# A two-layer diffusion backbone step: modulation loads on GpSimd's queue, one more modulation piece as VectorE sums, and eight instead of seven products in three groups of layer 0's MLP

## The chip, the cores and the metric

The kernel runs on one core of a Trainium2 chip. The metric is the device time of one execution in microseconds, the median over several runs.

## What is computed

The reference is one inference step through two post-norm layers, in float32, for 128 context tokens and 512 latent tokens (five tiles of 128) of width 1024:

```python
mod = silu(c) @ w_mod[l] + b_mod[l]          # 1024 -> 6 x 1024, one vector for latent, one for context tokens
sh1, sc1, g1, sh2, sc2, g2 = split(mod, 6)
u = x * (1 + sc1) + sh1
m = mixer(u)                                 # in-projection; SSD scan | short conv | differential attention; out-projection
x = layer_norm(ALPHA * x + g1 * m)
h = x * (1 + sc2) + sh2
f = square(relu(h @ w_up)) @ w_down          # 1024 -> 4096 -> 1024
x = layer_norm(ALPHA * x + g2 * f)
```

The six parts of `mod` are called pieces 0 to 5. Piece 5 is `g2`, the gate of the MLP's output, and is needed first when a layer's last MLP group is summed up. A layer's pieces 0 and 1 are needed before its in-projection, pieces 3 and 4 before its MLP.

## The kernel before

Every product of activations and weights is made in three float32r products: both operands are split into a rounded high part and a rest, and high x high, low x high and high x low are added in PSUM. For weights, ScalarE writes the high part and VectorE the rest (`split_unit`, L351); the activations lie transposed as `XH` and `XL`, eight row blocks by 640 tokens.

The code is written as straight Python over layers, groups and tiles. A framework turns it into one fixed order per engine: it takes, for each engine, the instruction of the best priority among those ready in its own estimate of the times, and puts in the waits. Priority is the place in the program, moved back by `LATE` = 100 places inside `high_priority(offset=-LATE)`. On the chip each engine and each DMA queue (SP's, ScalarE's, GpSimd's) then goes through its list in order.

**Modulation in layer 0.** Pieces 0 and 1 of layer 0 are made at the start. `mod_steps` (L186) makes pieces 2 to 5 of layer 0 (`PIECES`) on TensorE beside the z, sa and sb projections (the gate stage): per step two row blocks of `w_mod` are loaded (`wm`, 512 KB each, SP's queue, L200) and multiplied with a 32-column stationary operand. A piece has four such steps, and three for its tail (`mod_tail`, L160: copy, four transposes to a column layout, bias; after pieces 2 and 5 a transpose and a DMA of the gate to `gdram`).

**Modulation in the MLPs.** `mod_steps_sum` (L219) makes pieces 0 to 4 of layer 1 beside layer 0's MLP, and piece 5 of layer 1 beside layer 1's (`PIECES_MLP`). Here VectorE does the work: each of eight row blocks k and two column halves is loaded as `ws` (128x512, 256 KB, ring of 3, L232, SP's queue) and for each of the two token kinds added to a sum with the conditioning value as a per-partition scalar (L248; ScalarE for k = 0, L246). Four matmuls with ones close a piece over the partitions (L253), and `mod_tail` follows. A piece takes 19 steps, and one step of loads stands before the first piece. The sums `ma` are a ring of two, which the gate rows `grow` (L1147) use too.

**The pace.** `fill` takes steps from the list `fillers`. `spread(n)` (L268) adds n to an account and takes its whole part. It is called once for each of the 17 evacuations of the gate stage with `FZ` = 2.6, and in the MLP for each of 8 evacuations of an up-projection with `FU` = .6 and each of 10 of a down-projection with `FD` = 1.2. What is left is taken by `fill_all` in `before_last` (L1435).

**The MLP.** The 4096 hidden columns go in eight groups of 512 (L1450). Group 0 uses `up_block` (L1255): a plain product, 4 column tiles x 2 token halves x 8 row blocks x 3 = 192 matmuls of 320 tokens. Groups 1 to 7 use `fast_pair` (L1328) twice: seven products in place of eight (the Strassen-Winograd scheme on halves of rows and tokens), 2 x 7 x 4 x 3 = 168 matmuls. It forms differences of weights on VectorE and splits seven operands of 128x512 per pair, where a plain block splits four units of 128x1024 in all; its results are put together with three more VectorE adds per pair. The sums of tokens that it multiplies are made once (`token_sums`, L1289), and one quarter of `XH` and `XL` is overwritten by a difference (`token_sums_in_place`, L1310) after group 0's `up_block`, which needs the old content. Each group then has its down-projection (`dn_block`, L1404), 120 matmuls of 512 columns over four PSUM banks. In layer 0 ScalarE copies each result to a `part` buffer (ring of 3) and a DMA on GpSimd's queue adds it to `acc` (L1486); in layer 1 VectorE adds it from PSUM (L1489). Weight units live in a ring of five (`hi`, `lo`), their raw loads in a ring of three on SP's queue (L348, L1337).

`before_last` runs after the first pair of group 7: it takes all remaining steps, asks for the gate rows on GpSimd's queue (L1148), multiplies `acc` by them and adds the saved residual (L1439 to L1443).

Of the kernel before, what the change touches and what calls it, by code (L numbers as in the profile page):

```python
# [16 lines left out]
P = 128  # L17
# [15 lines left out]

RK, RZ, RY, RS, RW = 4, 4, 1.5, 2, 1

FZ, FU, FD = 2.6, .6, 1.2

PIECES, PIECES_MLP = (2, 3, 4, 5), (tuple((1, i) for i in range(5)), ((1, 5),))

DF, EK = 3, 2  # L40

# [17 lines left out]
def build(ctx: ExitStack, tc: tile.TileContext, I, O):  # L59
    nc = tc.nc  # L60
    V, S, G, T = nc.vector, nc.scalar, nc.gpsimd, nc.tensor
# [157 lines left out]
    def mod_steps_sum(pieces, pool):  # L219

        loads = [(l, pc, k, h) for l, pc in pieces for k in range(KT) for h in range(2)]
        got = {}

        def small(name):
            return pool.tile([P, 512], F32, tag="ws", name=name, bufs=3)

        def load():
            if loads:
                l, pc, k, h = at = loads.pop(0)
                w = got[at] = small(f"ws{l}_{pc}_{k}_{h}")  # L230
                c0 = pc * 1024 + h * 512
                nc.sync.dma_start(out=w, in_=I["w_mod"][l, k * P:(k + 1) * P, c0:c0 + 512])  # L232

        for _ in range(3):
            load()
        yield
        for l, pc in pieces:
            acc = [pool.tile([P, 1024], F32, tag="ma", name=f"ma{l}_{pc}_{s}", bufs=2) for s in range(2)]
            for k in range(KT):
                for h in range(2):  # L240
                    w = got.pop((l, pc, k, h))
                    with tc.high_priority(offset=-LATE):
                        for s in range(2):
                            a = acc[s][:, h * 512:(h + 1) * 512]
                            if k == 0:
                                act(a, w, scale=cst_c[:, k, s:s + 1])  # L246
                            else:
                                stt(a, w, cst_c[:, k, s:s + 1], a, ALU.mult, ALU.add)  # L248
                    load()
                    yield  # L250
            ps = ps_tp(f"pmod{l}_{pc}")
            for g in range(4):
                mm(ps[32 * g:32 * g + 32, :], one, acc[g // 2][:, (g % 2) * 512:(g % 2 + 1) * 512], True, True)  # L253
            yield from mod_tail(l, pc, ps, small(f"mrow{l}_{pc}"), False)
            yield
# [12 lines left out]
    def spread(n):  # L268
        due[0] += n
        fill(int(due[0]))  # L270
        due[0] -= int(due[0])
# [344 lines left out]
    for l in range(DEPTH):  # L616
# [131 lines left out]
        k = k_tile(NT)  # L748
# [506 lines left out]
        def up_block(g, b, ah, al):  # L1255
            blk = load_block(f"up{l}_{g}_{b}", w_up, 0, [(g * hg + b * 512, 512)])

            def ev_up(ct, half, ps):
                nm = f"relu{l}_{g}_{b}_{ct}_{half}"
                o, m, r = half * H, H, room(nm)  # L1260
                squared(r, ah[4 * b + ct][:, o:o + m], al[4 * b + ct][:, o:o + m], ps)
                spread(FU)

            ch_block(f"up{l}_{g}_{b}", blk, ev_up, na=H)

# [62 lines left out]
        def fast_pair(g, j, ah, al):  # L1328

            i = 2 * j  # L1330
            nm = f"{l}_{g}_{j}"
            c0 = g * hg + i * P
            raw = []
            for k in range(2):
                r = raw_tile(f"rup{nm}_{k}").rearrange("p (k c) -> p k c", k=4)
                src = w_up[512 * k:512 * k + 512, c0:c0 + 256]
                nc.sync.dma_start(out=r, in_=src.rearrange("(k p) c -> p k c", p=P))  # L1337
                raw.append(r)
            b11, b12, b21, b22 = (raw[k][:, :, P * c:P * c + P] for k in range(2) for c in range(2))
            w = {}  # L1340

            def unit(n, pool, bufs, t):
                return [pool.tile([P, n, 512], F32R, tag=x, name=f"{x}{nm}_{t}", bufs=bufs)
                        .rearrange("p i (k c) -> p i k c", k=4) for x in (("hi", "lo") if n == 2 else ("h1", "l1"))]

            b = unit(2, wp, 5, "b")
            for e, (n, x) in enumerate((("B11", b11), ("B21", b21))):
                act(b[0][:, e], x)
                tt(b[1][:, e], x, f(b[0][:, e]), ALU.subtract)
                w[n] = b[0][:, e], b[1][:, e]  # L1350
            t1, t2, t3, t4 = (flat(f"t{nm}_{i}").rearrange("p (a b) -> p a b", a=4) for i in range(4))
            sums = {"T1": (t1, b12, b11), "T2": (t2, b22, t1), "T3": (t3, b22, b12), "T4": (t4, b21, t2)}
            for ns in (("T2", "T1"), ("T3", "T4")):
                b = unit(2, wp, 5, ns[0])
                for n in sorted(ns):
                    tt(*sums[n], ALU.subtract)
                for e, n in enumerate(ns):
                    act(b[0][:, e], sums[n][0])
                    tt(b[1][:, e], sums[n][0], f(b[0][:, e]), ALU.subtract)
                    w[n] = b[0][:, e], b[1][:, e]  # L1360
            b = unit(1, op, 2, "c")
            act(b[0][:, 0], b22)
            tt(b[1][:, 0], b22, f(b[0][:, 0]), ALU.subtract)
            w["B22"] = b[0][:, 0], b[1][:, 0]

            def product(ps, wn, xn, more=False):

                for k in range(4):
                    wh, wl = (x[:, k] for x in w[wn])
                    xh, xl = quarter[xn](k)  # L1370
                    T.matmul(ps, lhsT=wh, rhs=xh, start=k == 0 and not more, stop=False, skip_group_check=more)  # L1371
                    T.matmul(ps, lhsT=wh, rhs=xl, start=False, stop=False, skip_group_check=more)  # L1372
                    T.matmul(ps, lhsT=wl, rhs=xh, start=False, stop=k == 3, skip_group_check=more)  # L1373

            def out(r, ct, half, src=None):
                spread(FU)
                o = H * half
                squared(r, ah[i + ct][:, o:o + H], al[i + ct][:, o:o + H], src)

            def bank(p, n):  # L1380
                return p(n + nm)[:, :H]


            px, pz, py = bank(ps_mm, "px"), bank(ps_tp, "pz"), ps_b2(f"py{nm}")[:, 0, :H]
            s1, p5, u = room("s1" + nm), flat("p5" + nm)[:, :H], room("u" + nm)
            product(px, "B11", "A11")
            act(s1, px)
            product(pz, "T1", "S1")
            act(p5, pz)
            product(px, "T2", "S2", True)  # L1390
            act(u, px)
            product(pz, "B22", "S4", True)
            tt(u, u, pz, ALU.add)
            out(u, 1, 0)
            product(px, "T3", "S3", True)
            tt(p5, p5, px, ALU.add)
            out(p5, 1, 1)
            product(py, "B21", "A12")
            tt(s1, s1, py, ALU.add)
            out(s1, 0, 0)  # L1400
            product(px, "T4", "A22", True)
            out(room("c21" + nm), 0, 1, px)
# [47 lines left out]
        for g in range(ng):  # L1450
            ah, al = a_tiles(g, hg // P)
            if g == 1:
                fillers.append(mod_steps_sum(PIECES_MLP[l], op))
            if g:
                for j in range(2):
                    fast_pair(g, j, ah, al)
                    if g == ng - 1 and j == 0:
                        before_last()
            else:
                for b in range(hg // 512):  # L1460
                    up_block(g, b, ah, al)
                    if g == 0 and b == 0:
                        with tc.high_priority(offset=-LATE):
                            for t, mv in later:
                                affine(rows, t, mv)
                                G.dma_start(out=mid[l][t * P:(t + 1) * P, :], in_=res[t])
                        rp_end.close()
                        sp, sp_end = open_pool("sp", "right")
                        with tc.high_priority(offset=-LATE):
                            token_sums()  # L1470
                token_sums_in_place()
            for cbi in range(2):
                blk = load_block(f"dn{l}_{g}_{cbi}", w_down, g * hg, [(cbi * 512, 512)], nu=hg // 256)
                cs = slice(cbi * 512, (cbi + 1) * 512)
# [4 lines left out]
                def ev_dn(t, ps, cbi=cbi, cs=cs, g=g):  # L1479
                    if g == 0:  # L1480
                        act(acc[t][:, cs], ps)
                        spread(FD)
                    elif g < ng - 1 and not end:
                        part = op.tile([P, 512], F32, tag="part", name=f"part{l}_{g}_{cbi}_{t}", bufs=3)
                        act(part, ps)
                        G.dma_start(out=acc[t][:, cs], in_=part, accum_op=ALU.add)  # L1486
                        spread(FD)
                    elif g < ng - 1:
                        tt(acc[t][:, cs], acc[t][:, cs], ps, ALU.add)  # L1489
                        spread(FD)  # L1490
                    else:
                        quiet = end and t in order[:-1]
                        residual(t, cbi, ps, None, not quiet)
# [86 lines left out]
```

## Time and profile before

| | |
|---|---|
| runs | 1637.12, 1631.19, 1635.31 us; median 1635.31 |
| the profiled execution | 1628.37 us |
| its span, first to last instruction | 1626.6 us, mean granted TensorE clock 0.995 |
| busy | TensorE 1563.3 us (96%), VectorE 1203.7 (74%), ScalarE 883.2 (54%), GpSimd 109.1 (7%) |
| layer 0: gate stage, out-projection, MLP begin at | 210.0, 341.4, 395.6 us |
| layer 1: gate stage, MLP begin at | 1040.3, 1183.6 us |

PE is TensorE's matmuls and PEld its weight loads, DVE VectorE, ACT ScalarE, POOL GpSimd, SP the queue of SyncE. Matmuls overlap, so the time of one step is read from the distance of two starts, not from the duration of a row. "x -> y" in a row names the tile written and the tiles read (out<-in), and L with a number the line of the kernel; helpers such as `mm` (L112), `act` (L97), `tt` (L100) and `stt` (L109) give one line to many places, so that tiles tell them apart. In a row of a wait, the engine and line that waited stand first, and after the arrow what released it.

### The profile page before, as it was taken

What the parts mean: (1) busy time and instruction counts of PE and PEld (TensorE: products, weight loads), DVE (VectorE), ACT (ScalarE), POOL (GpSimd) and SP (SyncE); (2) the same over time, 40 slices, a digit from 0 to 9 for tenths busy, and PEclk for the clock granted to TensorE, in tenths of its full rate; (3) what the DMA queues carried; (4) which work ended last, traced back from release to release, by engine and by line L of the source; (5) the groups of instructions that cost most, each with busy time, mean ns of one, the idle gap of its engine ahead of it and who ended that gap; (6) DMA issues with size and microseconds to landing.
All of it is one profiled execution on the core that took longest, in us unless ns stands there. A gap on an engine that the chain in (4) does not pass through costs nothing.

```text
span 1626.6 us, 24095 instructions
## 1 busy us (share of the span) xinstructions
PE 1563.3 (96%) x8944; PEld 1352.6 (83%) x8944; DVE 1203.7 (74%) x2216; ACT 883.2 (54%) x1886; POOL 109.1 (7%) x162
## 2 busy tenths in 40 slices
PE   6999999999999999898999999999999999999997
PEld 3799956787988888788887999798798889988985
DVE  2588865678994877667587788898799665565677
ACT  3368743436665465465455577564486355434543
POOL 0000000001002211210300000000000000000011
PEclk9999999999999999999999999999999999999999
DMA  9641177543256866774735510524334243122332
GB/s 323 176 163 53 53 249 256 183 151 139 79 182 143 226 178 168 192 186 142 185 130 169 197 40 14 181 98 148 112 133 131 81 130 90 66 69 88 104 113 81
DMA packets 142533, 227.71 MB, mean 140 GB/s; under 512 B 12236, under 2 KB 73424, under 8 KB 142416
## 3 DMA queue, kind: packets, MB, share of 16 engines
q1 hardware_dynamic: 122608, 179.46, 34.5%
q0 software_dynamic: 12256, 28.32, 7.8%
q10 hardware_dynamic: 7552, 18.40, 3.1%
q8 instruction: 70, 1.15, 0.3%
q14 instruction: 47, 0.39, 0.1%
HBM read 191.95 MB, written 18.46 MB: 129 GB/s over the span
## 4 chain that ended last, share of the span: by engine, by line
PE 59%; issue 22%; DVE 8%; DMA 4%; POOL 3%; ACT 3%; SPq 1%; POOLq 0%; DVEq 0%; ACTq 0%
PE dn_t L112 13%; PE wo_t L112 5%; PE sa_c L112 4%; PE xb_c L112 3%; PE kv_t L112 3%; PE z_t L112 3%; POOL acc L1486 3%; PE pt L112 2%; PE pmod L112 2%; PE xa_c L112 2%; PE px L1371 2%; PE px L1372 2%; PE px L1373 2%; PE dq_t L112 2%; PE sb_c L112 1%
## 5 line engine op out<-in xcount | busy, mean ns | idle before, releaser
L112 PE MATMUL dn_t<-hdn,al 128*128 128x512 f32 x640 | 252.0, 394 | 0.8 <-DVE al L100 0.8
L112 PE MATMUL dn_t<-hdn,ah 128*128 128x512 f32 x640 | 252.1, 394 | 0.0
L112 PE MATMUL dn_t<-ldn,ah 128*128 128x512 f32 x640 | 251.4, 393 | 0.0
L112 PEld LDWEIGHTS dn_t<-hdn,ah 128*128 128x128 f32 x640 | 120.1, 188 | 29.4 <-issue 0.8
L112 PEld LDWEIGHTS dn_t<-hdn,al 128*128 128x128 f32 x640 | 120.2, 188 | 28.3 <-DVE al L100 1.1
L112 PEld LDWEIGHTS dn_t<-ldn,ah 128*128 128x128 f32 x640 | 120.2, 188 | 27.4
L109 DVE SCALAR_TENSOR_TENSOR ma<-ws,cstat,ma 128x512 f32<-128x512 f32 x168 | 118.9, 748 | 28.6 <-DMA ws<-in_w_mod_dram 21.3
L100 DVE TENSOR_TENSOR ldn<-rdn,hdn 128x1024 fp32r<-128x1024 f32 x64 | 78.0, 1222 | 30.6 <-ACT hdn L97 30.5
L97 ACT ACTIVATE hi_T<-t 128x512 fp32r<-128x512 f32 x112 | 67.2, 626 | 56.7 <-DVE t L100 33.6
L100 DVE TENSOR_TENSOR lo_T<-t,hi_T 128x512 fp32r<-128x512 f32 x112 | 73.9, 687 | 30.2 <-ACT hi_T L97 30.1
L100 DVE TENSOR_TENSOR acc<-acc,dn_t 128x512 f32<-128x512 f32 x80 | 54.1, 684 | 49.6 <-PE dn_t L112 49.4
L1371 PE MATMUL px<-XH,hi_T 128*128 128x320 f32 x224 | 71.4, 319 | 12.6 <-ACT u L97 10.0
L97 ACT ACTIVATE hi_b<-rup 128x512 fp32r<-128x512 f32 x56 | 33.3, 623 | 78.2 <-PE dn_t L112 71.3
L97 ACT ACTIVATE hdn<-rdn 128x1024 fp32r<-128x1024 f32 x64 | 67.0, 1050 | 16.2 <-PE px L1372 13.7
L1486 POOL DMA_DIRECT2D acc<-part x60 | 51.3, 907 | 334.1 <-ACT part L97 253.3
L1372 PE MATMUL px<-XL,hi_T 128*128 128x320 f32 x224 | 69.7, 311 | 0.0
L1373 PE MATMUL px<-XH,lo_T 128*128 128x320 f32 x224 | 69.6, 310 | 0.0
L97 ACT ACTIVATE part<-dn_t 128x512 f32<-128x512 f32 x60 | 34.8, 595 | 63.0 <-PE dn_t L112 44.0
L112 PE MATMUL wo_t<-hwo,XH 128*128 128x512 f32 x160 | 63.8, 398 | 1.5 <-ACT XH L97 1.5
L112 PE MATMUL wo_t<-hwo,XL 128*128 128x512 f32 x160 | 63.6, 397 | 0.0
L112 PE MATMUL wo_t<-lwo,XH 128*128 128x512 f32 x160 | 63.2, 395 | 0.0
L97 ACT ACTIVATE pe<-sc,zs 128x640 f32<-128x640 f32 (+1 forms) x80 | 56.8, 711 | 7.5 <-DVE ams L106 3.1
(419 smaller groups left out, 4603.8 us busy)
## 6 DMA issues: line engine op xcount, KB each, us to landing
rup<-in_w_up_dram SPq DMA_DIRECT2D x64, 512.0 KB
rdn<-in_w_down_dram SPq DMA_DIRECT2D x64, 512.0 KB
ws<-in_w_mod_dram SPq DMA_DIRECT2D x96, 256.0 KB
wm<-in_w_mod_dram SPq DMA_DIRECT2D x32, 512.0 KB
acc<-part POOLq DMA_DIRECT2D x60, 256.0 KB, 4.6
Ab<-adram SPq DMA_DIRECT2D x10, 1024.0 KB
rwo<-in_w_out_dram SPq DMA_DIRECT2D x16, 512.0 KB
wb<-in_w_mod_dram SPq DMA_DIRECT2D x12, 512.0 KB
```

Source lines behind the costliest of these rows:

```text
L97: S.activation(out=out, in_=in_, func=func, **kw)
L100: V.tensor_tensor(out=out, in0=a, in1=b, op=op)
L109: V.scalar_tensor_tensor(out=out, in0=a, scalar=s, in1=b, op0=op0, op1=op1, **kw)
L112: T.matmul(out, lhsT=l, rhs=r, start=start, stop=stop)
L1371: T.matmul(ps, lhsT=wh, rhs=xh, start=k == 0 and not more, stop=False, skip_group_check=more)
L1372: T.matmul(ps, lhsT=wh, rhs=xl, start=False, stop=False, skip_group_check=more)
L1373: T.matmul(ps, lhsT=wl, rhs=xh, start=False, stop=k == 3, skip_group_check=more)
L1486: G.dma_start(out=acc[t][:, cs], in_=part, accum_op=ALU.add)
```

## The change

Three things change. The `ws` loads go out on GpSimd's queue. Piece 5 of layer 0 leaves `PIECES` and becomes the first piece that `mod_steps_sum` makes beside layer 0's MLP. And in layer 0 groups 1 to 3 use `up_block`; `fast_pair` begins at group 4 (`FAST`), and the in-place difference is made in group 3. The paces depend on the group: 1.3 per evacuation before `FAST[l]` and .65 from there on, for up and down alike; `FZ` is 2.

```diff
-FZ, FU, FD = 2.6, .6, 1.2
-
-PIECES, PIECES_MLP = (2, 3, 4, 5), (tuple((1, i) for i in range(5)), ((1, 5),))
+FZ, FU, FD = 2, (1.3, .65), (1.3, .65)
+
+FAST = (4, 1)
+
+PIECES, PIECES_MLP = (2, 3, 4), (((0, 5),) + tuple((1, i) for i in range(5)), ((1, 5),))
...
@@ mod_steps_sum
-                nc.sync.dma_start(out=w, in_=I["w_mod"][l, k * P:(k + 1) * P, c0:c0 + 512])
+                G.dma_start(out=w, in_=I["w_mod"][l, k * P:(k + 1) * P, c0:c0 + 512])
...
@@ up_block's ev_up, fast_pair's out
-                spread(FU)
+                spread(FU[g >= FAST[l]])
...
@@ the loop over groups
-            if g:
+            if g >= FAST[l]:
                 for j in range(2):
                     fast_pair(g, j, ah, al)
...
-                token_sums_in_place()
+                if g == FAST[l] - 1:
+                    token_sums_in_place()
...
@@ ev_dn, three places
-                        spread(FD)
+                        spread(FD[g >= FAST[l]])
```

## Rows read from the trace of the kernel before

**Rows 1.** The page's chain that ended last, by engine

```profile
PE 59%; issue 22%; DVE 8%; DMA 4%; POOL 3%; ACT 3%; SPq 1%; POOLq 0%; DVEq 0%; ACTq 0%
```

**Rows 2.** Windows (PE, PEld, DVE, ACT, POOL busy; clock): both gate stages

```profile
210.00:331.40 121.40, 121.40 (x651) 80.17 (x650) 74.06 (x180) 48.79 (x124) 2.77 (x5) 1.00 0.65 217
1040.30:1119.00 78.70, 78.70 (x504) 74.58 (x503) 72.61 (x170) 44.92 (x115) 3.39 (x5) 1.00 0.30 108
```

**Rows 3.** Timeline of PE in layer 0's gate stage (start, duration)

```profile
214.72 0.39 PE L112 MATMUL z_t<-hz,XH 128*128 128x512 f32 x1
214.95 0.40 PE L112 MATMUL z_t<-hz,XL 128*128 128x512 f32 x1
215.28 1.05 PE L112 MATMUL pmod<-wm,cstat 128*32 128x512 f32 x4
216.26 0.50 PE L112 MATMUL z_t<-lz,XH 128*128 128x512 f32 x1
```

**Rows 4.** Windows: layer 0's down 0, groups 1-6; layer 1's groups 2, 3

```profile
427.40:455.30 27.90, 27.90 (x122) 22.43 (x121) 26.29 (x53) 16.90 (x33) 0.00 (x0) 1.00 0.37 113
455.30:509.70 54.40, 53.41 (x290) 47.16 (x289) 36.60 (x60) 28.81 (x58) 7.80 (x9) 1.00 0.64 166
509.70:564.00 54.30, 54.30 (x302) 47.77 (x301) 43.58 (x71) 32.14 (x63) 8.54 (x10) 1.00 0.77 198
564.00:618.30 54.30, 54.30 (x302) 47.80 (x301) 40.24 (x65) 32.50 (x63) 8.52 (x10) 1.00 0.73 188
618.30:676.60 58.30, 55.00 (x303) 47.66 (x302) 39.01 (x67) 32.48 (x64) 8.50 (x10) 1.00 0.69 173
676.60:735.70 59.10, 55.06 (x302) 47.60 (x301) 42.24 (x69) 32.25 (x63) 8.53 (x10) 1.00 0.72 184
735.70:796.30 60.60, 56.14 (x302) 48.89 (x301) 37.34 (x64) 29.32 (x59) 9.68 (x12) 0.97 0.61 157
1297.30:1351.10 53.80, 53.80 (x303) 47.77 (x302) 31.71 (x53) 25.27 (x50) 1.07 (x2) 1.00 0.31 98
1351.10:1403.20 52.10, 52.10 (x290) 47.16 (x289) 31.36 (x51) 24.14 (x48) 0.00 (x0) 1.00 0.27 81
```

**Rows 5.** Waits from 618 to 797 us (total, times, longest)

```profile
DVE ma L109 <- DMA ws<-in_w_mod_dram: 12.5, 10, 3.1
...
PEld px L1371 <- ACT u L97: 10.3, 3, 4.7
```

**Rows 6.** Timeline of group 6's start, VectorE, then PE

```profile
742.27 3.40 DVE L109 SCALAR_TENSOR_TENSOR ma<-ws,cstat,ma 128x512 f32<-128x512 f32 x5
...
747.32 0.63 PE L1371 MATMUL px<-XH,hi_T 128*128 128x320 f32 x1 [4.44 <-ACT u L97]
```

**Rows 7.** Waits of SP's queue, 427 to 618, then 618 to 800 us

```profile
SPq L232 <- DVE ma L109: 59.5, 37, 6.4
...
SPq L232 <- DVE ma L109: 51.7, 27, 8.9
```

**Rows 8.** Timeline of PE in layer 0's up block of group 0

```profile
405.44 0.31 PE L112 MATMUL up_c<-XL,hup 128*128 128x320 f32 x1
...
407.35 0.31 PE L112 MATMUL up_c<-XH,lup 128*128 128x320 f32 x1
```

**Rows 9.** The page's costliest groups: sums, split remainders, layer 1's adds

```profile
L109 DVE SCALAR_TENSOR_TENSOR ma<-ws,cstat,ma 128x512 f32<-128x512 f32 x168 | 118.9, 748 | 28.6 <-DMA ws<-in_w_mod_dram 21.3
L100 DVE TENSOR_TENSOR ldn<-rdn,hdn 128x1024 fp32r<-128x1024 f32 x64 | 78.0, 1222 | 30.6 <-ACT hdn L97 30.5
...
L100 DVE TENSOR_TENSOR acc<-acc,dn_t 128x512 f32<-128x512 f32 x80 | 54.1, 684 | 49.6 <-PE dn_t L112 49.4
```

**Rows 10.** The page's group and DMA issues of the adds

```profile
L1486 POOL DMA_DIRECT2D acc<-part x60 | 51.3, 907 | 334.1 <-ACT part L97 253.3
...
acc<-part POOLq DMA_DIRECT2D x60, 256.0 KB, 4.6
```

**Rows 11.** Timeline of GpSimd at the end of group 6

```profile
784.51 1.31 POOL L1148 DMA_DIRECT2D grow<-gdram  x2
```

More of the change, by code (lines that the diff above doesn't have):

```diff
@@ L1375, in out @@
             def out(r, ct, half, src=None):
-                spread(FU)
+                spread(FU[g >= FAST[l]])
                 o = H * half
@@ L1486, in ev_dn @@
                         G.dma_start(out=acc[t][:, cs], in_=part, accum_op=ALU.add)
-                        spread(FD)
+                        spread(FD[g >= FAST[l]])
                     elif g < ng - 1:
                         tt(acc[t][:, cs], acc[t][:, cs], ps, ALU.add)
-                        spread(FD)
+                        spread(FD[g >= FAST[l]])
                     else:
```

## The prediction, made blind

> **What bounds the kernel now.** I read the page's chain first: of what ended last, 59% is PE and 22% "issue", most of it between PE's own instructions [rows 1]. So a change pays where it takes columns off TensorE or ends one of its few waits, and costs where it adds columns. Next I read the windows of the two stages that the diff touches.
>
> In layer 0's gate stage (z, sa, sb) TensorE is busy for 121.40 us of 121.40; layer 1's same stage, with no modulation in it, takes 78.70, also full [rows 2]. The 42.7 us between them are the four pieces of PIECES, 10.7 us each. The timeline shows why: one step of a piece starts behind a z matmul that began at 214.95 and lets the next begin at 216.26, 1.31 us later, where neighbours stand 0.23 apart [rows 3]: 1.08 us on TensorE for half a step (four of its eight matmul records). A piece has eight such halves and a tail of transposes.
>
> In layer 0's MLP each row is one group of up and down [rows 4]. Groups 2 and 3 take 54.3 us each with TensorE always busy. Group 1 takes 54.4 with 1.0 us idle. Groups 4 to 6 take 58.3, 59.1 and 60.6, with 3.3, 4.0 and 4.5 us idle, and the granted clock is 0.97 in the last. Layer 1 gives the clean values: 52.10 for a fast group, 53.80 for one that holds a piece's closing sums, so those cost 1.7 us on TensorE. Layer 0's 54.3 less 1.7 is 52.6 clean. Groups 4 to 6 hold one closing each, so 178.0 us contain 178.0 - 3 x 54.3 = 15.1 us of loss; group 1 adds 1.8. These 16.9 us are all that better order could bring there.
>
> The waits name the loss. From 618 to 797, TensorE's weight loads wait 10.3 us for ACT's u, and VectorE waits 12.5 us for ws loads [rows 5]. The timeline of group 6 shows it as one chain: five weighted sums run on VectorE from 742.27 to 745.67, ahead of the weight differences that ACT must split before it reads u; TensorE then starts at 747.32 after 4.44 us idle [rows 6]. Groups 2 and 3 hid as much VectorE work (43.58 and 40.24 us) as groups 4 to 6 lost time with (39.01, 42.24, 37.34) [rows 4]. So it is the order and the late ws loads, not VectorE's total, that lose.
>
> **The change part by part.**
>
> *One piece leaves TensorE's gate stage.* The prices above bound it at -8.6 (eight times 1.08, no tail) and -10.7 (the mean of four). I take -10.2, nearer the mean because the tail goes too. TensorE stays full without it, since the stage still stands over layer 1's 78.70 [rows 2]. FZ drops from 2.6 to 2, but 21 steps now end in the 11th call, as 28 did, so the pace costs nothing. SP loses eight wm loads; below that I price nothing.
>
> *It returns as weighted sums.* Seven rows of weights by two halves by two streams are 28 VectorE instructions of 748 ns [rows 9], 20.9 us, with four on ACT, 16 ws loads, and 1.7 us of closing sums on TensorE. A piece has 19 steps, so six make 115 with the first. Groups 1 to 3 issue 18 x 1.3 = 23.4 steps each, groups 4 to 6 18 x 0.65 = 11.7 (16.8 before), and group 7's first pair 2.6: 107.9, leaving some 7 to the fill before the last group.
>
> *Groups 1 to 3 take eight products.* Thirteen matmul steps span 405.44 to 407.35 in group 0, 0.147 us each [rows 8]. An up block has 192, so 28.1 us; with group 0's down stretch of 27.9 [rows 4] a group is 56.0. Pieces end at steps 20, 39, 58, 77, 96 and 115, so three closings fall here: 3 x 56.0 + 3 x 1.7 = 173.1 against 163.0 now. That is **+10.1** (group 1 to 3 today from 455.3 to 618.3). What covers the weighted sums: a fast group in layer 1 has 31.36 us of VectorE with ten 684 ns adds, 24.5 without them; the eight-product group has eight splits of 1222 ns, 9.8, and eight narrower subtractions, under 5.5 [rows 4, 9]. With 23.4 x 28/19 = 34.5 sums, 25.8 us, that is 41 us of 56. They lie beside. If an up block's fourth weight unit comes late, TensorE stands: its slot frees some 1.4 us before the down stretch ends and it is wanted 2.6 us after; a split of 1.2 us on each of ACT and VectorE fits, a queue of three sums before it does not. Bounds 0 to 2 us a group.
>
> *token_sums_in_place moves from group 0 to group 3.* Sixteen VectorE operations of 320 columns, under 0.684 us each, so under 10.9, in a down stretch of 27.9; group 3 would be at 52 of 56. Group 0 is relieved of as much (26.29 of 27.90 now [rows 4]) and gains nothing, as its TensorE is full. Cost 0, up to 3.
>
> *Groups 4 to 6 get 11.7 steps.* Clean: 3 x 52.6 + 2 x 1.7 = 161.2 against 178.0, **-16.8** with no loss left. VectorE then holds 24.5 + 17.2 x 0.748 = 37.4 us in 52.6, less than groups 2 and 3 hid.
>
> *The ws loads move to GpSimd's queue.* SP now waits 59.5 and 51.7 us in two stretches for a sum to free a ws slot [rows 7], with weight loads queued behind; that goes. Behind them on GpSimd now stand the adds acc<-part, 60 at 907 ns, landing 4.6 us after issue [rows 10]. For GpSimd's price of a load the add is the nearest row: some 20 loads and 10 adds are 27 us of 56 in groups 1 to 3, a free engine. What a delayed add costs is the third rival.
>
> The Trainium skill ("SBUF — State Buffer", "SBUF: two separate sides") warns that GpSimd cannot write its DMA descriptors while VectorE runs a two-port copy, and gives 620 ns grown to 3100. By that page's figures, as an estimate, 20 loads a group would hold GpSimd 50 us longer, and the third rival would be the outcome, at a higher price. The trace does not agree so far: 60 adds beside a VectorE that is 60 to 80% busy average 907 ns [rows 4, 10], and the sums read two tensors. So the page moves no chance here.
>
> *Group 7.* The sixth closing, +1.7. The gate rows share a ring with the sums and were asked for at 784.51, 11.8 us before group 7 [rows 11]; now they wait for the sixth piece.
>
> *Layer 1.* Piece (1,5) at .65 instead of .6 and 1.2: it ends in the same group or the next; 0, bounds -1 to +1.
>
> **The sum.** -10.2 + 10.1 - 16.8 + 1.7 = -15.2 if no wait is left. I keep a third of today's 16.9 us of loss, 5.7, as the loads are freed and the sums thinned to 0.7 but stay static in order: -9.5. The profiled execution, 1628.37 with a span of 1626.6, becomes 1618.9; it lies 6.9 under the median, and at the median the forecast is **1625.8** (-0.58%). A difference under 0.5% (8.2 us) can't be told from none.
>
> **The rivals.**
>
> *The loss stays (0.25).* If VectorE's order makes it and not SP, each step keeps its price, 15.1 / 50.4 = 0.30 us: 35.1 steps lose 10.5, the start 1.8, and the sum is -2.9, 1632.4; with the whole 16.9 it is +1.7, 1637.0. For it: the sums stood in a block in [rows 6], whatever queue fed them. Against: VectorE's 12.5 us waiting for ws [rows 5], and groups 2 and 3. The Trainium skill ("DMA: Bandwidth & Descriptors", "Issuing engines are not separate DMA queues") says that another issuing engine saves only issue time, which would make the move worth nothing; [rows 7] show a queue standing behind a slot instead, so I give it only this chance.
>
> *The gate rows come late (0.07).* Five steps' sums, 7.5 us, run in group 7's up block beside the fifteen operations of the residual. Past the 11.8 us of head start they delay the last down stretch by up to 7: 1632.8.
>
> *GpSimd's queue becomes the bound (0.14), slower.* A ws load that waits for its slot holds the adds behind it. Three part buffers at one eviction per 2.8 us last 8.4; eviction, issue and landing take 6.1, so 2.3 us are spare, and a PSUM bank gives 2.8 more. The longest waits for a slot were 6.4 and 8.9 us [rows 7]. From 5.1 us on, ACT stands in order at part, the up splits behind it are late, and TensorE waits: about 4 us a group, more where it recurs. Six groups cost 24, the sum is +14.5, 1649.8. Against it: adds come only in down stretches, and the loads' slots free sooner when VectorE is idle.
>
> **How the numbers follow.** Forecast 0.54, loss stays 0.25, gate rows 0.07, queue 0.14. Faster is the forecast; same holds the second and third; slower the last. The low end is no loss left with the best bounds, -19, 1616. The high end takes in the second and third rival and the cheaper part of the last, 1645.
>
> **What would show it.** Right: the gate stage near 111 us, still full; groups 1 to 3 at 56 to 59; groups 4 to 6 at 52.6 to 55 with TensorE's wait for u down from 10.3 to 3. Wrong: ACT's part waiting for acc<-part in tens of us, idle TensorE at the starts of groups 2 to 4, or a last down stretch that waits for the residual's operations on VectorE.

## The result, and the profile after

The changed kernel takes 1655.3 us (median of four runs, 1654.95 to 1664.03) against 1634.7 of the kernel before: the ratio is 1.0137, with a 95% interval of 1.0118 to 1.0157. It is slower by 1.4%, and outside the range of the prediction. The span of its profiled execution is 1653.2 us, 26.6 more than before. Between the medians the difference is 20.6 us, because the profiled execution of the kernel before, at 1628.37, was one of its faster ones; a few us of the differences by stage are of that kind.

The first fence has windows of the changed kernel: the stretch from the first z matmul to the first of the out-projection, then groups 1 to 3, 4 to 6 and 7 of layer 0's MLP, the last up to layer 1's first kv matmul. The columns are those of [rows 2, 4]. The second has the same first and last stretch of the kernel before; groups 1 to 6 of before are in [rows 4]. In the kernel before z's first matmul starts at 188.25 and the out-projection's first at 332.85, so this stretch is longer than the one in [rows 2].

```profile
188.73:315.11 126.38, 124.84 (x740) 95.83 (x738) 94.49 (x211) 62.12 (x153) 5.97 (x15) 1.00 0.63 211
...
437.70:626.80 189.10, 178.93 (x975) 157.87 (x974) 103.23 (x157) 85.44 (x152) 48.29 (x72) 0.96 0.62 163
626.80:807.50 180.70, 167.06 (x890) 146.84 (x889) 121.35 (x197) 95.34 (x186) 47.70 (x68) 0.96 0.68 170
807.50:880.80 73.30, 59.17 (x325) 51.37 (x325) 53.12 (x93) 35.04 (x67) 9.01 (x16) 0.91 0.41 129
```

```profile
188.25:332.85 144.60, 143.40 (x778) 98.24 (x776) 94.93 (x213) 62.97 (x155) 4.56 (x12) 1.00 0.64 211
...
796.30:856.40 60.10, 57.28 (x313) 50.70 (x312) 50.50 (x86) 33.91 (x65) 7.95 (x14) 0.97 0.44 140
```

Against before, the changed kernel stands as follows, in us:

| stretch | before | after | difference | forecast, no loss left | with the loss kept |
|---|---|---|---|---|---|
| up to group 1's start | 455.3 | 437.7 | -17.6 | -10.2 | -10.2 |
| groups 1 to 3 | 163.0 | 189.1 | +26.1 | +10.1 | +10.1, its loss in the next row |
| groups 4 to 6 | 178.0 | 180.7 | +2.7 | -16.8 | -11.1, with both rows' loss |
| group 7 to layer 1 | 60.1 | 73.3 | +13.2 | +1.7 | +1.7 |
| layer 1 | 770.2 | 772.4 | +2.2 | 0 | 0 |
| sum | 1626.6 | 1653.2 | +26.6 | -15.2 | -9.5 |

The gate stage went from 144.6 to 126.4, a gain of 18.2 us where 10.2 were priced. The MLP of layer 0 lost 42.0 us where a gain of 5 was summed up with no loss left, and a loss of 0.7 with a third of it kept.

**The gate stage.** The timeline of PE shows two full steps standing in a row, and one step in a row at another place:

```profile
251.73 1.07 PE L114 MATMUL pmod<-wm,cstat 128*32 128x512 f32 x8
252.73 0.38 PE L114 MATMUL sa_c<-XH,hsa 128*128 128x256 f32 x1
...
265.03 1.92 PE L114 MATMUL pmod<-wm,cstat 128*32 128x512 f32 x16
266.88 0.39 PE L114 MATMUL sa_c<-XH,hsa 128*128 128x256 f32 x1
```

From the start of the sixteen pmod records to the next matmul's are 1.85 us, 0.116 a record, and from the start of the eight 1.00 us. In [rows 3] a row of four, half a step, already takes 0.98 us (215.28 to 216.26), 0.25 a record. So a step that is cut in two by z's matmuls costs nearly twice what an uncut one does. In the kernel before one step in eight stands uncut; with FZ = 2 five of the twelve that are left do.

**The start of an up block.** The waits of groups 1 to 3 (total, times, longest), and then the timeline of group 1, ScalarE's split of the fourth weight unit first, then VectorE, and PE behind the dots, with a window at the end:

```profile
DVE ma L111 <- DMA ws<-in_w_mod_dram: 21.3, 19, 3.5
...
ACT part L99 <- DMA acc<-part: 12.9, 8, 4.1
...
PE up_c L114 <- DVE lup L102: 10.1, 3, 6.3
```

```profile
436.30 1.06 ACT L99 ACTIVATE hup<-rup 128x1024 fp32r<-128x1024 f32 x1 [0.56 <-PE dn_t L114]
...
433.06 4.07 DVE L111 SCALAR_TENSOR_TENSOR ma<-ws,cstat,ma 128x512 f32<-128x512 f32 x6 [2.38 <-DMA ws<-in_w_mod_dram]
...
437.89 3.68 DVE L111 SCALAR_TENSOR_TENSOR ma<-ws,cstat,ma 128x512 f32<-128x512 f32 x5 [0.36 <-DMA ws<-in_w_mod_dram]
441.49 1.22 DVE L102 TENSOR_TENSOR lup<-rup,hup 128x1024 fp32r<-128x1024 f32 x1
...
442.76 0.42 PE L114 MATMUL up_c<-XH,lup 128*128 128x320 f32 x1 [1.94 <-DVE lup L102]
...
445.33 0.47 PE L114 MATMUL up_c<-XL,hup 128*128 128x320 f32 x1
445.60 0.47 PE L114 MATMUL up_c<-XH,lup 128*128 128x320 f32 x1
...
443.46:446.66 3.20, 3.20 (x14) 3.20 (x13) 3.20 (x8) 1.38 (x3) 0.54 (x1) 0.50 0.78 272
```

Sums run on VectorE to 437.1 after a wait of 2.38 us for a ws load, then five more from 437.89. Only then comes lup, the rest of the up block's fourth and last weight unit, though ScalarE has its hup ready at 437.36. PE stands for 1.94 us and goes on at 442.76. From 443.46 its matmuls start 0.27 us apart where 0.147 is the rule [rows 8]: the granted clock is 0.50 there, its lower level of 1.2 GHz, for more than 3 us. This stop of 2 us so costs 3.7 by the time the old spacing is back. Group 2 has the same stop with 1.87 us, and group 3 with 6.30, the longest in the waits:

```profile
568.26 0.75 DVE L111 SCALAR_TENSOR_TENSOR ma<-ws,cstat,ma 128x512 f32<-128x512 f32 x1 [1.25 <-DMA ws<-in_w_mod_dram]
568.93 1.22 DVE L102 TENSOR_TENSOR lup<-rup,hup 128x1024 fp32r<-128x1024 f32 x1
...
570.20 0.64 PE L114 MATMUL up_c<-XH,lup 128*128 128x320 f32 x1 [6.30 <-DVE lup L102]
```

The three stops are 10.1 us of the three groups' 189.1. TensorE is busy for 178.9, which is 5.8 more than the 173.1 of the prediction, at a mean granted clock of 0.96.

**Groups 4 to 6.** PE's longest stops are the kind that [rows 6] show, and one for the gate of a closed piece:

```profile
640.80 0.63 PE L1373 MATMUL px<-XH,hi_T 128*128 128x320 f32 x1 [6.84 <-ACT u L99]
675.57 0.37 PE L184 MATMUL pmg<-ident,modT 128*16 128x128 f32 x1 [3.37 <-DVE modT L102]
```

TensorE's weight loads wait 10.0 us for u here, against 10.3 before [rows 5].

**Group 7.** GpSimd's, VectorE's and PE's timelines:

```profile
821.41 1.11 POOL L1150 DMA_DIRECT2D grow<-gdram  x2 [1.33 <-PE pmod L114]
...
825.80 1.23 DVE L102 TENSOR_TENSOR acc<-acc,grow 128x1024 f32<-128x1024 f32 x1 [2.35 <-DMA grow<-gdram]
...
835.50 2.48 DVE L111 SCALAR_TENSOR_TENSOR acc<-x,acc 128x512 f32<-128x512 f32 x4
837.90 0.68 DVE L102 TENSOR_TENSOR t<-rup 128x512 f32<-128x512 f32 x1
...
839.30 0.64 PE L1373 MATMUL pz<-Sh,hi_T 128*128 128x320 f32 x1 [14.09 <-ACT hi_T L99]
```

The gate rows are asked for at 821.41, 14 us into the group; before they were asked for 11.8 us ahead of it [rows 11]. VectorE multiplies and adds with them until 838, and only then forms the second pair's weight differences. PE stands for 14.09 us.

**The queue.** Groups and DMA issues of the page:

```profile
L111 DVE SCALAR_TENSOR_TENSOR ma<-ws,cstat,ma 128x512 f32<-128x512 f32 x196 | 138.1, 746 | 53.5 <-DMA ws<-in_w_mod_dram 43.4
...
L234 POOL DMA_DIRECT2D ws<-in_w_mod_dram x112 | 64.0, 574 | 264.9 <-DVE ma L111 165.3
...
ws<-in_w_mod_dram POOLq DMA_DIRECT2D x112, 256.0 KB, 4.0
```

VectorE's idle time for ws loads has doubled, from 21.3 to 43.4 us [rows 9], although the sums are only a sixth more. A ws load costs GpSimd 574 ns and lands 4.0 us after its issue.

### The profile page after: what moved, and what is told of

The parts are those of the page before. It is cut to its first block, busy times and chain, and to the rows that moved or that the text cites. A ratio compares the mean times of both kernels' runs of the same rounds, so it can differ in the third digit from the quotient of the medians.

```text
span 1653.2 us, 24121 instructions
## 1 busy us (share of the span) xinstructions
PE 1565.9 (95%) x8992; PEld 1369.5 (83%) x8992; DVE 1189.1 (72%) x2172; ACT 873.0 (53%) x1842; POOL 171.3 (10%) x274
## 5 line engine op out<-in xcount | busy, mean ns | idle before, releaser
L111 DVE SCALAR_TENSOR_TENSOR ma<-ws,cstat,ma 128x512 f32<-128x512 f32 x196 | 138.1, 746 | 53.5 <-DMA ws<-in_w_mod_dram 43.4
L114 PE MATMUL up_c<-XH,lup 128*128 128x320 f32 x320 | 101.2, 317 | 10.1 <-DVE lup L102 10.1
L114 PE MATMUL up_c<-XL,hup 128*128 128x320 f32 x320 | 100.9, 316 | 1.2 <-DVE XL L102 1.1
L114 PE MATMUL up_c<-XH,hup 128*128 128x320 f32 x320 | 101.2, 316 | 0.2
L234 POOL DMA_DIRECT2D ws<-in_w_mod_dram x112 | 64.0, 574 | 264.9 <-DVE ma L111 165.3
L99 ACT ACTIVATE hi_T<-t 128x512 fp32r<-128x512 f32 x88 | 52.6, 625 | 60.1 <-DVE t L102 33.0
L102 DVE TENSOR_TENSOR lo_T<-t,hi_T 128x512 fp32r<-128x512 f32 x88 | 57.5, 685 | 22.6 <-ACT hi_T L99 22.5
L114 PEld LDWEIGHTS up_c<-XH,lup 128*128 128x128 f32 x320 | 61.6, 193 | 10.9 <-DVE lup L102 10.9
L1373 PE MATMUL px<-XH,hi_T 128*128 128x320 f32 x176 | 56.1, 319 | 11.8 <-ACT u L99 9.9
L99 ACT ACTIVATE hi_b<-rup 128x512 fp32r<-128x512 f32 x44 | 26.3, 624 | 74.3 <-PE dn_t L114 69.1
```

The costliest lines, as they stand in the source:

```text
L99: S.activation(out=out, in_=in_, func=func, **kw)
L102: V.tensor_tensor(out=out, in0=a, in1=b, op=op)
L111: V.scalar_tensor_tensor(out=out, in0=a, scalar=s, in1=b, op0=op0, op1=op1, **kw)
L114: T.matmul(out, lhsT=l, rhs=r, start=start, stop=stop)
L234: G.dma_start(out=w, in_=I["w_mod"][l, k * P:(k + 1) * P, c0:c0 + 512])
```

## The experiments

Each kernel was timed against the kernel before on the same chip, and its ratio to that is given. Those that ran once have one time and no interval. Windows are cut as above: gate stage (z to out-projection), groups 1 to 3, groups 4 to 6, group 7.

### after_sp: the loads back on SP's queue

```diff
@@ the changed kernel, mod_steps_sum
-                G.dma_start(out=w, in_=I["w_mod"][...
+                nc.sync.dma_start(out=w, in_=I["w_mod"][...
```

> The changed kernel with its ws loads back on SP's queue. If GpSimd's queue is what costs (loads and adds in one line), groups 1 to 6 of layer 0's MLP fall from 369.8 us by 15 or more, and the time from 1655 to 1640 or less. If VectorE's order at the start of an up block costs, whatever queue feeds the sums, the time stays within 5 us of 1655 and TensorE's first waits for lup stay at 2 to 6 us a group.

Measured: 1646.93 us, ratio 1.0089 (1.0069 to 1.0110). Groups 1 to 3 and 4 to 6:

```profile
438.90:622.70 183.80, 176.22 (x974) 155.77 (x973) 101.32 (x152) 85.37 (x152) 24.88 (x29) 0.98 0.63 170
622.70:797.40 174.70, 166.59 (x890) 146.84 (x889) 120.21 (x197) 95.91 (x185) 25.71 (x30) 0.96 0.66 172
```

Groups 1 to 6 went from 369.8 to 358.5, so 11.3 of the 15 that the queue theory wanted, and the time fell by 8.4 where the other theory allowed 5. So GpSimd's queue has a part of some 8 us in the changed kernel, 0.5% by the two ratios. Most of the loss stayed with the queue gone: in groups 1 to 3 TensorE still waits 7.6 us for lup.

### before_fz2: the kernel before with whole steps in pairs

```diff
-FZ, FU, FD = 2.6, .6, 1.2
+FZ, FU, FD = 2, .6, 1.2
```

> The kernel before with FZ = 2 instead of 2.6 and nothing else. If the gate stage's surplus (18 us won where 10.2 were priced) comes from steps that now stand in a row on TensorE, at 0.20 us a pmod record instead of 0.27, the stage falls from 121.4 to about 112 and the time to about 1626. If only the number of pieces counts, the stage stays at 121 and the time at 1635.

Measured: 1622.85 us, ratio 0.9950 (0.9928 to 0.9972). The gate stage:

```profile
190.70:327.60 136.90, 134.53 (x778) 97.86 (x776) 95.22 (x213) 63.02 (x155) 4.59 (x12) 1.00 0.65 223
```

It fell from 144.6 to 136.9, by 7.7 us. Added up from the start of each row of pmod to the next matmul's, the 128 records hold TensorE for 0.21 us each instead of 0.27, which is 7.2 us of it. The ratio, 0.5%, says as much. The pace of whole steps is a gain by itself.

### seven: seven products everywhere, one even pace

```diff
@@ the changed kernel
-FZ, FU, FD = 2, (1.3, .65), (1.3, .65)
+FZ, FU, FD = 2, (1.07, 1.07), (1.07, 1.07)
-FAST = (4, 1)
+FAST = (1, 1)
```

> The changed kernel with seven products in groups 1 to 3 again and one pace of 1.07 in all groups (115.6 steps by the end of group 6). If an up block's last weight unit, late behind sums on VectorE, is what costs, groups 1 to 3 fall from 189 us to 165 to 172 and the time to about 1632 to 1640. If the VectorE work of the sixth piece is what costs, the six fast groups lose it instead and the time stays at 1650 or more.

Measured: 1609.39 us, ratio 0.9858 (0.9840 to 0.9875), better than the forecast for it. All four stretches:

```profile
189.02:315.39 126.37, 124.72 (x740) 95.73 (x738) 94.54 (x211) 62.18 (x153) 4.60 (x12) 1.00 0.61 209
438.50:605.70 167.20, 165.21 (x903) 142.87 (x902) 122.98 (x201) 95.56 (x189) 48.49 (x72) 1.00 0.71 187
605.70:773.50 167.80, 165.02 (x904) 142.91 (x903) 128.05 (x216) 95.62 (x189) 51.67 (x77) 1.00 0.75 196
773.50:835.40 61.90, 58.83 (x313) 51.94 (x312) 52.84 (x89) 33.96 (x66) 7.94 (x14) 0.94 0.46 142
```

The gain of the gate stage stays (126.4), groups 1 to 6 take 335.0 against 341.0 of before though they make a piece more, and group 7 is back near 60. VectorE carries more here (123 and 128 us) than in the changed kernel (103 and 121), so its total is not what cost. This run changes the products and the pace at once; "even" below parts them.

### pace_end: all steps done before group 7

```diff
@@ the changed kernel
-FZ, FU, FD = 2, (1.3, .65), (1.3, .65)
+FZ, FU, FD = 2, (1.4, .8), (1.4, .8)
```

> The changed kernel with paces 1.4 and .8, so that all 115 steps are issued before group 7 (118.8). If the gate rows that wait for the sixth piece cost group 7 its 13 us, the stretch from group 7's start to the next layer falls from 73.3 to about 61, and the time to 1642 to 1648, less what groups 4 to 6 lose to the quicker pace. If group 7 is slow for another cause, the stretch stays at 73.

Measured: 1621.65 us, ratio 0.9931 (0.9912 to 0.9950). Groups 1 to 3, 4 to 6 and 7:

```profile
438.10:624.00 185.90, 177.26 (x982) 155.43 (x980) 111.73 (x172) 84.97 (x152) 51.87 (x80) 0.98 0.65 176
624.00:787.10 163.10, 162.38 (x894) 143.15 (x894) 114.80 (x188) 94.93 (x186) 45.02 (x63) 1.00 0.71 183
787.10:848.60 61.50, 58.79 (x313) 52.18 (x312) 49.56 (x86) 33.92 (x65) 7.93 (x14) 0.94 0.42 137
```

Group 7 fell from 73.3 to 61.5, as the gate rows' theory had it. What no theory had: groups 4 to 6 fell too, from 180.7 to 163.1, with more steps in them. The fixed order came out with hardly a stop there (162.38 of 163.10 busy). Groups 1 to 3 stay at 186, at 25.2 steps a group.

### few_sums: an eighth of the sums

```diff
@@ the changed kernel, mod_steps_sum
-        loads = [(l, pc, k, h) for l, pc in pieces for k in range(KT) for h in range(2)]
+        loads = [(l, pc, k, h) for l, pc in pieces for k in range(1) for h in range(2)]
...
-            for k in range(KT):
+            for k in range(1):
```

> The changed kernel, but the weighted sums beside the MLPs take only the first of eight row blocks (k = 0, on ScalarE), so pieces (0,5) and (1,0) to (1,5) are made of an eighth of their products and loads; all else stands. If sums on VectorE that wait for their loads hold up an up block's last weight unit, the up blocks of groups 1 to 3 fall from 31.9, 31.8 and 37.2 us to about 28.1 (plus 1.7 where a piece closes), with no wait of TensorE for lup. If the ring of five weight units alone makes that unit late, the blocks stay at 31 or more.

This kernel leaves out seven of the eight row blocks, so its modulation is not that of the reference.

Measured: 1607.04 us in a single run. Groups 1 to 3 and 4 to 6:

```profile
437.50:616.10 178.60, 178.60 (x1011) 155.26 (x1010) 49.22 (x83) 91.53 (x164) 29.99 (x38) 1.00 0.50 126
616.10:774.00 157.90, 157.90 (x865) 141.53 (x864) 77.40 (x122) 89.15 (x174) 25.74 (x30) 1.00 0.55 130
```

TensorE is always busy from group 1 to group 6. With pieces of five steps, six closings fall into groups 1 and 2: 178.6 - 6 x 1.7 = 168.4, which is 56.1 a group against the 56.0 of the prediction. The last three take 52.6 each, as it said. The ring of five weight units alone holds nothing up.

### no_loads: all sums, no late loads

```diff
@@ the changed kernel, mod_steps_sum
-                w = got[at] = small(f"ws{l}_{pc}_{k}_{h}")
...
+                if len(kept) < 2:
+                    w = pool.tile([P, 512], F32, tag="wk", name=f"ws{l}_{pc}_{k}_{h}", bufs=2)
...
+                    kept.append(w)
+                got[at] = kept[h]
```

> The changed kernel with all its weighted sums, but only the first two blocks of modulation weights are loaded and every sum reads one of them, so that no sum waits for a load; the other loads are left out. If the sums' waits for late loads make the blocks that hold up the weight units, groups 1 to 3 fall from 189 us to 171 to 176 and groups 4 to 6 from 180.8 to 162 to 168. If the amount of VectorE work in a fixed order does it, groups 1 to 3 stay above 182.

This kernel leaves out all but the first two loads and sums those again and again.

Measured: 1629.31 us in a single run. Groups 1 to 3, 4 to 6 and 7:

```profile
442.70:616.20 173.50, 173.50 (x975) 153.62 (x974) 97.05 (x145) 85.71 (x152) 24.93 (x29) 1.00 0.47 113
616.20:780.30 164.10, 162.12 (x891) 142.51 (x890) 116.43 (x193) 94.98 (x185) 25.79 (x30) 1.00 0.53 126
780.30:854.20 73.90, 59.34 (x326) 51.52 (x324) 53.12 (x93) 35.12 (x67) 9.11 (x16) 0.91 0.41 128
```

Groups 1 to 3 take 173.5 us with TensorE always busy; the prediction's price was 173.1. VectorE does nearly as much as in the changed kernel there (97 us of 103). So it is not the work but the loads. They act in ways that this run does not part: sums wait for them (2.38 and 0.36 us ahead of group 1), the order comes out otherwise, and their traffic and their place in GpSimd's queue are gone too. As to the order: in the changed kernel sixteen sums stand between the third and the fourth lup of group 1, here nine, and lup is ready by 443.6 for a group that starts at 442.7. Group 7 keeps its 73.9, since the gate rows still wait for the sixth piece.

### before_eight: eight products alone

```diff
@@ the kernel before, the loop over groups
-            if g:
+            if g >= FAST[l]:
...
-                token_sums_in_place()
+                if g == FAST[l] - 1:
+                    token_sums_in_place()
```

> The kernel before with eight products in groups 1 to 3 of layer 0 and nothing else (old paces, four pieces on TensorE, loads on SP). Columns alone make groups 1 to 3 173 us against 163.0, and the time 1640 to 1645. If sums in front of an up block's last weight unit are the larger part of the loss, TensorE waits for lup here too and groups 1 to 3 take 178 or more, the time 1647 or more.

Measured: 1648.01 us, ratio 1.0077 (1.0060 to 1.0095). Groups 1 to 3 and 4 to 6:

```profile
457.70:629.50 171.80, 171.80 (x962) 153.28 (x961) 82.25 (x123) 80.34 (x144) 23.96 (x28) 1.00 0.59 154
629.50:810.10 180.60, 166.44 (x902) 144.41 (x901) 123.03 (x204) 95.63 (x189) 27.64 (x33) 0.98 0.70 176
```

At 16.8 steps a group the eight products cost their columns and no stop: 171.8 us, always busy, 8.8 above before. The time came out higher than the 1640 to 1645 that went with that: it is 11.4 us above the median of the kernel before on the same chip (1636.62). Between the profiled executions groups 4 to 6 differ by 2.6 us, the way up to group 1 by 2.4 and layer 1 by 4.3 as well, none of which the edit touches. The eight products do not make the stop, then; with them, more steps a group do. Seven products at 23.4 steps were not run.

### even: eight products at an even pace

```diff
@@ the changed kernel
-FZ, FU, FD = 2, (1.3, .65), (1.3, .65)
+FZ, FU, FD = 2, (1.07, 1.07), (1.07, 1.07)
```

> The changed kernel with an even pace of 1.07 in all groups (19.3 steps a group instead of 23.4 and 11.7), eight products in groups 1 to 3 as before it. If the quick pace of groups 1 to 3 is what makes the loads late, those groups fall from 189 us to 172 to 178, group 7's stretch to about 62, and the time to 1616 to 1624. If eight products and sums do not go together at any such pace, groups 1 to 3 stay above 182.

Measured: 1623.70 us, ratio 0.9934 (0.9911 to 0.9957). Groups 1 to 3, 4 to 6 and 7:

```profile
438.50:619.30 180.80, 177.04 (x975) 155.99 (x973) 93.55 (x141) 83.31 (x151) 44.77 (x66) 0.98 0.63 163
619.30:788.30 169.00, 164.98 (x904) 142.86 (x902) 127.74 (x216) 95.52 (x188) 51.40 (x76) 1.00 0.76 195
788.30:849.30 61.00, 57.60 (x313) 51.06 (x313) 52.80 (x89) 33.81 (x65) 7.97 (x14) 0.97 0.45 143
```

Groups 4 to 7 did as the pace theory had it. Groups 1 to 3 came out between the two theories, at 180.8: 19.3 steps a group still lose 7.7 us there over the price of 173.1. Against "seven", which differs from it by the products alone, it is 14 us slower.

### The queue in two other kernels: seven_sp and before_g

```diff
@@ seven_sp: the kernel "seven", mod_steps_sum
-                G.dma_start(out=w, in_=I["w_mod"][...
+                nc.sync.dma_start(out=w, in_=I["w_mod"][...
@@ before_g: the kernel before, mod_steps_sum
-                nc.sync.dma_start(out=w, in_=I["w_mod"][...
+                G.dma_start(out=w, in_=I["w_mod"][...
```

> The kernel with seven products everywhere and a pace of 1.07, with its ws loads on SP's queue. If GpSimd's queue costs as it did in the changed kernel (8 us), groups 1 to 6 fall from 334.9 us and the time from 1609 to about 1601. If the free queue helps where every group has the same pace, the time rises to 1613 or more. Within 3 us: the queue does not matter here.

Measured: 1608.30 us, ratio 0.9836 (0.9795 to 0.9878), not told apart from "seven". Groups 1 to 6 take 333.0 us.

> The kernel before with only the ws loads on GpSimd's queue. If SP's waits for ws slots (111 us in all, with weight loads behind them) were what made groups 4 to 6 lose 15 us, those fall from 178.0 to 165 to 170 and the time from 1631 to 1621 to 1626. If only VectorE's fixed order made the loss, it stays within 4 us of 1631. If the adds behind the loads hold ScalarE, it is 1640 or more.

Measured: 1638.41 us, ratio 1.0012 (0.9991 to 1.0034). Groups 4 to 6 of before_g:

```profile
621.10:801.70 180.60, 169.48 (x902) 148.64 (x901) 121.12 (x197) 94.60 (x186) 47.92 (x68) 0.96 0.67 171
```

Groups 4 to 6 of before_g take 180.6 with SP free of the loads, so SP's waits did not make the loss of 15 us. The time of 1640 or more that was named for ScalarE held up by the adds did not come either.

### The gate stage's pace: after_fz26 and seven_fz4

```diff
@@ after_fz26: the changed kernel
-FZ, FU, FD = 2, (1.3, .65), (1.3, .65)
+FZ, FU, FD = 2.6, (1.3, .65), (1.3, .65)
@@ seven_fz4: the kernel "seven"
-FZ, FU, FD = 2, (1.07, 1.07), (1.07, 1.07)
+FZ, FU, FD = 4, (1.07, 1.07), (1.07, 1.07)
```

> The changed kernel with FZ = 2.6. If its gate stage won 6 us beyond the piece because steps in pairs keep modulation matmuls together, the stretch from z to the out-projection grows from 124.9 to about 131, with pmod starts 0.25 us or more apart instead of 0.20. If not, it stays at 125.

Measured: 1665.06 us in a single run. The gate stage of after_fz26:

```profile
191.90:325.90 134.00, 132.95 (x740) 96.59 (x738) 94.66 (x210) 61.93 (x153) 6.99 (x15) 1.00 0.60 199
```

It grew from 126.4 to 134.1, by the same 7.7 us, with 0.27 us a pmod record again.

> The same kernel with FZ = 4 instead of 2, so that all four matmul steps of a piece stand in a row on TensorE. If longer rows of modulation matmuls run closer together, the time from z to the out-projection falls below 125.4 us by 2 to 5, and the total from 1609 to 1604 to 1607. If rows of two steps already have all of it, or the loads now hold TensorE, it stays at 1609 or rises.

Measured: 1626.26 us, ratio 0.9948 (0.9930 to 0.9967). The gate stage of seven_fz4:

```profile
190.30:332.10 141.80, 134.44 (x740) 98.89 (x738) 95.59 (x210) 62.16 (x153) 5.57 (x12) 0.96 0.55 186
```

The quick pace runs into loads that are not there yet (TensorE's weight loads wait 7.7 us for wm): TensorE is busy for 134.4 us of 141.8, the clock falls to 0.96, and 15.5 us of the stage are given back. Of the three paces tried, 2 is the best for this ring of loads.

## Why the prediction was wrong

- **The step that failed first** is the bound "0 to 2 us a group" for an up block whose fourth weight unit comes late. The prediction named the place, the slack and the danger ("a queue of three sums before it does not" fit), and then counted VectorE's load, 41 us of 56, as cover. Load is not cover where the order is fixed and each sum may wait for a DMA. With the columns at 173.1, as forecast (no_loads 173.5, before_eight 171.8 with two closings instead of three), the stops made it 189.1, 5.3 us a group: 10.1 of standing and 5.8 of slower matmuls. One of the prediction's own signs of being wrong came true, idle TensorE at the starts of groups 2 to 4.
- **Groups 4 to 6**: the clean price of 52.6 is right (few_sums), and pace_end comes to 163.1. That a slower pace thins the loss to a third was wrong as a rule: 11.7 steps gave 180.7, 14.4 gave 163.1, 19.3 gave 169.0. What decides, as far as pace_end and no_loads (164.1 at 11.7) show, is where the fixed order puts the sums and whether their loads are there. TensorE's wait for u, forecast to fall from 10.3 to 3 us, stayed at 10.0.
- **Group 7** was the second rival, with a chance of 0.07 and a price of at most 7 us. It came, and cost 13.2. The price took the fifteen residual operations to run beside the sums that were left; they stand ahead of the second pair's weights, so that the wait came in that pair and not in the last down stretch. pace_end and even take it away (61.5, 61.0).
- **The gate stage** gained 18.2 us against a price of 10.2. The price of the piece was right: 10.5 us with FZ = 2.6 in both kernels (144.6 to 134.1) and 10.5 with FZ = 2 (136.9 to 126.4). "The pace costs nothing" was the failing step: FZ = 2 is itself worth 7.7 us of this stage, in the kernel before (before_fz2) as in the changed one (after_fz26).
- **token_sums_in_place** was priced in group 3's down stretch. The order put the forming of its differences into group 1 (from 430.2 to 449.2) and only their writing into group 3. No run parts what that cost.
- **The third rival**, the adds held up behind loads on GpSimd, had the right sign for the wrong reason, and that its 1649.8 lies near the measured time is luck. ScalarE waits 12.9 us for the adds in groups 1 to 3 of the changed kernel, and 16.1 us did the same before; TensorE's stops come from VectorE. The queue's own part is 8 us, in the changed kernel alone. That another issuing engine by itself gains next to nothing is what the Trainium skill says ("DMA: Bandwidth & Descriptors", "Issuing engines are not separate DMA queues"); before_g and seven_sp agree with it, at ratios that are 0.1 to 0.2% from those on the other queue; the changed kernel, 0.5% slower on GpSimd's queue (after_sp), does not.
- Of the descriptors that VectorE could hold up (the Trainium skill, "SBUF — State Buffer", "SBUF: two separate sides") there is no sign: 112 loads were issued at 574 ns in the mean, less than the adds' 907 of before [rows 10].

What stays open is why one pace gives a good order and the next a bad one: the orders were read from the traces, and the estimate of times by which the framework makes them was not tried apart.

## What to carry to other kernels

Filler work on an engine with a fixed order is hidden only if its own inputs are surely there: count its waits for loads, place by place, and not its share of busy time. Test a change of several parts one by one: here two of them (the piece moved off TensorE, whole steps in pairs) are worth 1.4 to 1.6% with seven products kept and an even pace (1609.4 and 1608.3 us), while the eight products and the uneven pace turned that into a loss of 1.4%. What is made last should not hold a buffer that the next stage's first load needs.

## What the runs showed of the hardware

Modulation matmuls of 32 stationary columns, on four parts of the array, held TensorE for 0.98 us in a row of four between other matmuls ([rows 3]), for 1.00 us in a row of eight and for 1.85 in a row of sixteen. A stop of TensorE of 1.94 us was followed by more than 3 us at the lower clock, and one of 14.09 us lay in a stretch whose mean granted clock is 0.91.
